# Scan quarters cut into five held pieces, one convolution tile from TensorE to VectorE, and ordered steps in the closing norm

## The chip, the core and the metric

One core of a Trainium2 chip runs the whole program. The metric is device time in microseconds (us), the median of three runs. Engines are written PE (TensorE, matrix products), DVE (VectorE), ACT (ScalarE), POOL (GpSimd) and SP (SyncE, which issues the loads). SBUF is the on-chip memory of the operands; PSUM holds the banks into which TensorE adds.

## The reference, cut to what matters

512 positions, 1024 channels. A hybrid layer comes first (block 1), and a second block of two layers follows, which the change does not touch.

```python
proj = einsum("bld,de->ble", rms_norm(x, pre_g), w_in)
conv_in, z_c, u_s, z_s, g_c, g_s = split(proj)
cu = ca * sigmoid(cb)                        # conv_in in two halves, 1024 channels
cu = causal_depthwise_conv(cu, conv_w)       # 31 taps along the positions, per channel
cu = silu(layer_norm(cu))
conv_out = (cu * silu(z_c)) @ w_conv_out
y = gelu(s5_mimo(u_s, ...))                  # 32 groups: s_t = A s_{t-1} + B u_t, complex, 64 states
y = y * sigmoid(y @ w_glu + b_glu)
ssm_out = (y * silu(z_s)) @ w_ssm_out
merged = sigmoid(g_c) * conv_out + sigmoid(g_s) * ssm_out
out = x + rms_norm(merged @ w_out, post_g)
```

## The kernel before, in words

Everything is transposed: 128 channels stand on the partitions and the 512 positions along the free side, so 1024 channels are eight tiles. A float32 product of 128x128 by 128x512 is made of three matmuls (helper `mm3`, L247 to L249: high x by high w, low x by high w, high x by low w). So each weight chunk of 128x1024 is loaded by SP (`raw`), rounded by ScalarE (`wh`, L235), and the rest is taken by VectorE (`wl`, L236), in rings of two and three buffers. A step that projects one pair of channel tiles is two banks of 24 matmuls.

Block 1 is a list of steps in ORDER_A and then ORDER_B, strings of a letter and a number. `p` projects a pair and gates it into `cu`, the input of a convolution tile on ScalarE, GpSimd or VectorE. `P` projects the same and lays it out for TensorE (`vb`, `ca`, `cp`, `cph`, `cpl`; L694 to L722). `t` is the convolution of one tile on TensorE (`toeplitz`): four weight chunks, 96 matmuls of 128x256 into one bank. `c` is the convolution of one tile tap by tap: for tiles in CONV_POOL ScalarE multiplies (`cw`, L755) and GpSimd adds into `xa` (L756), 30 times; for others VectorE does one multiply-add for each tap. `u` projects the scan's input, `s` and `z` the gates' inputs. `T` makes the scan's tables on small tiles, `R` the rotations (L506 to L511, VectorE), `Q` the kernel matrices of one quarter of the groups (outer products on GpSimd, L529 and L532; transposes and products on TensorE, L542 and L551), `q` the scan of the quarter itself: `pv` from `us` (L581), `vs` rotated through a permutation on TensorE (L585), the scan on VectorE into `st` (L591), a second permutation (L593), `sh` (L599), and sixteen products `py` (L603, L604). After that come `L`, the layer norm over all eight convolved tiles, and `C`, the projection of the convolved branch.

The order of the instructions on each engine is settled when the program is built. A scheduler that works with costs of its own takes what is ready in the order of priorities; steps get theirs in the order of the string, and B1_PRIO adds 20000 to a `c` step, so that its taps go where an engine would else be free. On the chip each engine then works its list strictly in that order. A step that is late on one engine holds what stands behind it there.

The layer ends with a norm in halves of 256 positions: for each half eight `og` multiplies (L921), eight additions (L922), eight roundings `xh` (L924) and eight rests `xl` (L925), which the next block's first matmuls read; then sums of squares of the new `x` (ScalarE squares, GpSimd adds into `acc`), which the ones-matmul L277 turns into the next norm's factor.

Of the kernel before, what the change touches and what calls it, by code (L numbers as in the profile page):

```python
# [19 lines left out]
PI_C3 = float(np.float32(TWO_PI - PI_C1 - PI_C2))  # L20
PI_CLAMP = 3.1415925

CONV_PE = (1, 2, 4, 6, 7)
VEC = {}
_o = 0
for _n, _w in (
# [466 lines left out]
def s5_rot(P, tb):  # L493
    V = P.nc.vector
    c, s = (P.q4.tile([128, 2048], F32, name=n).rearrange("p (g k) -> p g k", g=32) for n in ("rc", "rsn"))
    V.memset(c[:, :, 0:1], 1.0)
    V.memset(s[:, :, 0:1], 0.0)
    ta, tb_ = P.t("ra"), P.t("rb")
    for i in range(6):
        m = 1 << i  # L500
        n = min(32, 512 // m)
        for g0 in range(0, 32, n):
            g = slice(g0, g0 + n)
            cq, sq = (a[:, g].unsqueeze(2).to_broadcast([128, n, m]) for a in tb["rot"][i])
# [6 lines left out]
            V.tensor_tensor(out=s[:, g, m:2 * m], in0=A, in1=B, op=ALU.add)  # L511
    tb["cs"] = c, s


def s5_pre(P, tb, q):
    nc = P.nc
    V, GP = nc.vector, nc.gpsimd

    def big(name, n=1024):
        return P.q4.tile([128, n], F32, name=name, bufs=1 if name == "t1" else 2)  # L520

    def outer(out, x0, p0, x1, p1, n0, n1):
        n = n1 - n0
# [36 lines left out]

def s5_main(P, tb, q, u_dram, y_dram):
    nc = P.nc
# [13 lines left out]
    def flat(a):  # L576
        return a.rearrange("p g k -> p (g k)")
# [45 lines left out]
def block1(P, nxt):  # L623
    nc, tc, ap = P.nc, P.tc, P.ap
    V, GP, A = nc.vector, nc.gpsimd, nc.scalar
    TT = V.tensor_tensor
    STT = V.scalar_tensor_tensor
    with ExitStack() as ctx:
# [31 lines left out]
        def proj(i):  # L660
            h, l = P.wload(ap["w_in"][i], 2048)
            out = []
            for a in range(2):
                ps = P.ps()
                P.mm3(ps, h, l, 1024 * a, P.xh, P.xl)
                out.append(ps)
            return out

# [56 lines left out]
        def toeplitz(k):  # L725
# [3 lines left out]
            for c in range(4):  # L729
                (h,), (l,) = P.wload(src[:, 1024 * c:1024 * c + 1024], 1024)  # L730
                g, s0 = c // 2, 8 * (c % 2)
                for i in range(8):
                    s = 16 - s0 - i
                    o = slice(128 * i, 128 * i + 128)
                    a, b = s0 + i == 0, s0 + i == 15
                    d = ps[:, 256 * g:256 * g + 256]
                    xh, xl = hi[:, g, s:s + 256], lo[:, g, s:s + 256]
                    nc.tensor.matmul(d, h[:, o], xh, start=a, stop=False)  # L738
                    nc.tensor.matmul(d, h[:, o], xl, start=False, stop=False)
                    nc.tensor.matmul(d, l[:, o], xh, start=False, stop=b)  # L740
# [6 lines left out]
            summed(k)  # L747

        def conv(k):
            cu, y = cus[k], yc[k]  # L750
            if k in CONV_POOL:
                A.activation(y, cu[:, 0:T], AF.Identity, scale=hcw[:, 31 * k:31 * k + 1], bias=P.v("conv_b", k))
# [102 lines left out]
        def cout(o):  # L855
# [9 lines left out]
        tb = {}  # L865
        step = {"p": pair, "c": conv, "P": phases, "t": toeplitz, "u": u_, "s": zs_, "z": zc_, "g": gate, "y": gelu,
                "Q": lambda q: s5_pre(P, tb, q), "q": lambda q: s5_main(P, tb, q, u_dram, y_dram),
                "T": lambda i: tb.update(s5_tables(P, None)), "R": lambda i: s5_rot(P, tb), "G": lambda i: glu(), "S": ssm, "L": lambda i: ln(),
                "C": cout}

# [46 lines left out]
        for st, s in zip(sts, HALVES):  # L917
            A.activation(sd[:, s], st[:, s], AF.Sqrt, scale=1.0 / D, bias=P.eps6)
            V.reciprocal(rp[:, s], sd[:, s])
            for k in range(8):  # L920
                TT(out=og[k][:, s], in0=og[k][:, s], in1=rp[:, s], op=ALU.mult)  # L921
                TT(out=P.x[k][:, s], in0=og[k][:, s], in1=P.x[k][:, s], op=ALU.add)  # L922
                g = gcol(P, *nxt, k)
                A.activation(P.xh[k][:, s], P.x[k][:, s], AF.Copy, scale=g)  # L924
                STT(out=P.xl[k][:, s], in0=P.x[k][:, s], scalar=g, in1=P.xh[k][:, s].bitcast(F32), op0=ALU.mult, op1=ALU.subtract)  # L925
        for k in range(8):
            acc = P.sumsq(P.x[k], acc)
        P.rs = P.rstd_of(acc)


# [3 lines left out]
def proj_first(P, src, xT, sqx):  # L934
# [33 lines left out]
    for a in range(2):  # L968
# [8 lines left out]
B1_CLASS = {"c": "C", "t": "V", "R": "T", "T": "T", "Q": "Q", "q": "S", "y": "S", "G": "S", "L": "L"}  # L977
# [1010 lines left out]
```

## Time and profile before

| what | us |
| --- | --- |
| median of three runs | 2697.33 (2696.21 to 2700.18) |
| profiled execution | 2696.53, its span 2694.8, granted clock 0.965 |
| TensorE busy in the span | 2553.4 (95%) |
| block 1, from the first tables to the z steps, 95.5 to 372.8 | 277.30, TensorE busy 201.72 |
| z, gates and projections, 372.8 to 609 | 236.20, TensorE busy 235.31 |
| closing norm and the first half banks behind it, 609 to 638 | 29.00, TensorE busy 21.83 |

A stage's length less TensorE's busy time is what TensorE waits for there. The profiled execution's own time is 1.7 us longer than its span and lies 0.8 below the median.

### The profile page before, as it was taken

The page shows a single profiled execution, that of the slowest core. Times are in us where ns is not written, and L with a number is a line of the kernel's source. Part 1 is how long each engine was busy: PE and PEld are TensorE (multiplying, and loading weights), DVE is VectorE, ACT ScalarE, POOL GpSimd, SP SyncE. Part 2 cuts the span into 40 slices and gives each one's busy share as a digit, 9 for nine tenths or more (in the row PEclk, how much of TensorE's full clock was granted, in tenths as well). Part 3 has the DMA queues.
Part 4 walks back from the last instruction along what each step waited for, and adds up shares of the span by engine and source line. Part 5 has one row for each costly group of instructions (what it writes and reads, how often), then busy time and mean ns, then how long its engine had stood idle before and what let it go on. Part 6 is the DMA issues. An engine that isn't in the chain of part 4 may idle for free.

```text
span 2694.8 us, 32197 instructions
## 1 busy us (share of the span) xinstructions
PE 2553.4 (95%) x12828; PEld 2080.7 (77%) x12828; DVE 1432.3 (53%) x1916; ACT 947.8 (35%) x1356; POOL 511.2 (19%) x362
## 2 busy tenths in 40 slices
PE   8578789998999999999999999999999988999999
PEld 6557678887888886688678888888888767788887
DVE  7875545738434458734464344443444776643442
ACT  6443434434222233322142232432233565432231
POOL 5876702011000055332010000100001231100000
PEclk9788889999999999999899999999999989999999
DMA  4222332332232342315122332332323422132323
GB/s 145 90 83 75 94 92 86 110 118 78 92 104 95 98 142 74 79 46 124 48 78 89 99 102 87 101 102 88 108 90 126 110 90 71 52 105 85 108 92 99
DMA packets 116807, 252.91 MB, mean 94 GB/s; under 512 B 44177, under 2 KB 53137, under 8 KB 116657
## 3 DMA queue, kind: packets, MB, share of 16 engines
q1 hardware_dynamic: 116512, 250.64, 29.6%
q8 instruction: 100, 1.64, 0.2%
q14 instruction: 51, 0.41, 0.1%
q10 hardware_dynamic: 144, 0.22, 0.0%
HBM read 236.26 MB, written 13.37 MB: 93 GB/s over the span
## 4 chain that ended last, share of the span: by engine, by line
PE 70%; DVE 4%; ACT 1%; issue 1%; DMA 0%; POOL 0%; POOLq 0%; ACTq 0%; DVEq 0%
PE bank L247 21%; PE bank L248 21%; PE bank L249 21%; PE bank L1863 1%; PE bank L1225 1%; PE bank L1421 1%; PE bank L1424 0%; PE bank L1361 0%; DVE xl L270 0%; PE bank L1288 0%; PE bank L1370 0%; PE bank L1301 0%; PE bank L1366 0%; DVE xl L925 0%; PE bank L1458 0%
## 5 line engine op out<-in xcount | busy, mean ns | idle before, releaser
L235 ACT CAST wh<-raw 128x1024 fp32r<-128x1024 f32 (+1 forms) x452 | 436.8, 967 | 1225.3 <-PE bank L248 884.9
L247 PE MATMUL bank<-xh,wh 128*128 128x512 f32 (+1 forms) x2152 | 838.0, 391 | 20.7 <-ACT xh L953 6.4
L248 PE MATMUL bank<-xl,wh 128*128 128x512 f32 (+1 forms) x2152 | 838.6, 390 | 4.6 <-DVE xl L925 3.1
L249 PE MATMUL bank<-xh,wl 128*128 128x512 f32 (+1 forms) x2152 | 837.2, 390 | 0.9 <-DVE wl L236 0.9
L236 DVE TENSOR_TENSOR wl<-raw,wh 128x1024 fp32r<-128x1024 f32 (+1 forms) x418 | 485.7, 1163 | 369.3 <-ACT wh L235 360.8
L247 PEld LDWEIGHTS bank<-xh,wh 128*128 128x128 f32 x2152 | 407.3, 190 | 112.9 <-issue 10.4
L248 PEld LDWEIGHTS bank<-xl,wh 128*128 128x128 f32 x2152 | 408.0, 190 | 92.0 <-DVE xl L954 4.3
L249 PEld LDWEIGHTS bank<-xh,wl 128*128 128x128 f32 x2152 | 408.0, 190 | 86.4 <-issue 3.3
L264 POOL TENSOR_TENSOR acc<-acc,sq 128x512 f32<-128x512 f32 x54 | 89.3, 1654 | 1376.2 <-ACT sq L263 1369.4
L248 PE MATMUL bank<-ml,wh 128*128 128x512 f32 x704 | 273.9, 389 | 0.0
L249 PE MATMUL bank<-mh,wl 128*128 128x512 f32 x704 | 273.9, 389 | 0.0
L247 PE MATMUL bank<-mh,wh 128*128 128x512 f32 x704 | 272.6, 389 | 0.0
L331 DVE TENSOR_TENSOR up<-bank,rs 128x512 f32<-128x512 f32 x88 | 60.8, 691 | 273.6 <-PE bank L249 273.6
L327 DVE TENSOR_TENSOR gp<-bank,rs 128x512 f32<-128x512 f32 x88 | 60.8, 691 | 177.4 <-PE bank L249 177.1
L247 PEld LDWEIGHTS bank<-mh,wh 128*128 128x128 f32 x704 | 132.1, 188 | 27.5
L248 PEld LDWEIGHTS bank<-ml,wh 128*128 128x128 f32 x704 | 132.1, 188 | 27.5
L249 PEld LDWEIGHTS bank<-mh,wl 128*128 128x128 f32 x704 | 132.1, 188 | 27.3
L756 POOL TENSOR_TENSOR xa<-xa,cw 128x512 f32<-128x512 f32 x90 | 136.9, 1522 | 45.9 <-ACT cw L755 42.6
L236 POOL TENSOR_TENSOR wl<-raw,wh 128x1024 fp32r<-128x1024 f32 x34 | 83.0, 2443 | 143.8 <-ACT wh L235 138.5
L738 PE MATMUL bank<-cph,wh 128*128 128x256 f32 x160 | 51.8, 324 | 41.0 <-ACT cph L721 41.0
L339 DVE SCALAR_TENSOR_TENSOR xa<-bank,xa 128x512 f32<-128x512 f32 x64 | 44.3, 692 | 79.8 <-PE bank L249 79.8
L755 ACT ACTIVATE cw<-cu,hcw 128x512 f32<-128x512 f32 x90 | 63.8, 719 | 49.3 <-POOL xa L756 49.2
(642 smaller groups left out, 2967.3 us busy)
## 6 DMA issues: line engine op xcount, KB each, us to landing
raw<-in_ffn_gu_dram SPq DMA_DIRECT2D x176, 512.0 KB, 3.4
raw<-in_ffn_dn_dram SPq DMA_DIRECT2D x64, 512.0 KB, 3.5
raw<-in_w_in_dram SPq DMA_DIRECT2D x46, 512.0 KB, 3.5
raw<-in_even_in_dram SPq DMA_DIRECT2D x26, 512.0 KB, 3.5
raw<-in_ffn_dn_dram SPq DMA_DIRECT2D x64, 192.0 KB, 2.3
raw<-in_conv_dram SPq DMA_DIRECT2D x20, 512.0 KB, 3.8
xa<-in_xT_dram SPq DMA_DIRECT2D x16, 256.0 KB, 4.4
raw<-in_w_co_dram SPq DMA_DIRECT2D x8, 512.0 KB, 3.3
```

Source lines behind the costliest of these rows:

```text
L235: nc.scalar.copy(h[:, :m], raw[:, :m])
L236: self.wlo.tensor_tensor(out=l[:, :m], in0=raw[:, :m], in1=h[:, :m].bitcast(F32), op=ALU.subtract)
L247: self.nc.tensor.matmul(ps, h[i][:, s], xh[k], start=a, stop=False)
L248: self.nc.tensor.matmul(ps, h[i][:, s], xl[k], start=False, stop=False)
L249: last = self.nc.tensor.matmul(ps, l[i][:, s], xh[k], start=False, stop=b)
L264: nc.gpsimd.tensor_tensor(out=acc, in0=acc, in1=sq, op=ALU.add)
L327: nc.vector.tensor_tensor(out=gp, in0=pg, in1=rs, op=ALU.mult)
L331: nc.vector.tensor_tensor(out=up, in0=pu, in1=rs, op=ALU.mult)
L339: nc.vector.scalar_tensor_tensor(out=P.x[o], in0=ps, scalar=0.5, in1=P.x[o], op0=ALU.mult, op1=ALU.add)
L738: nc.tensor.matmul(d, h[:, o], xh, start=a, stop=False)
L755: A.activation(w, cu[:, j:j + T], AF.Copy, scale=hcw[:, 31 * k + j:31 * k + j + 1])
L756: GP.tensor_tensor(out=y, in0=y, in1=w, op=ALU.add)
```

## The change

One tile leaves TensorE: tile 7 is convolved on VectorE, and so is tile 5, which was on ScalarE and GpSimd. GpSimd keeps tiles 0 and 3, TensorE 1, 2, 4 and 6. `Q` becomes `Q` (outer products) and `K` (transposes and products); `q` becomes `q` (to `vs`), `r` (to the scan), `x` (to `sh`) and `w` (`py` and out). Each piece but `Q` is given an order edge: on TensorE it stands behind the last matmul of the step that is written ahead of it (`P.last_mm`). A convolution on GpSimd gets an edge behind the last outer product, one on VectorE an edge behind the last rotation. In the norm the multiply of `og` for tile k stands behind `xl` of tile k-3, and the sums of squares behind the last `xh`. An order edge (`tc.issue_after`) fixes who stands first in one engine's list; it is no wait between engines.

```diff
-CONV_PE = (1, 2, 4, 6, 7)
+CONV_PE = (1, 2, 4, 6)
...
-CU_BUFS = 2
-CONV_POOL = (0, 3, 5)
+CU_BUFS = 4
+CONV_POOL = (0, 3)
...
-            GP.tensor_tensor(out=o, in0=o, in1=tmp, op=ALU.add)
+            P.last_gp = GP.tensor_tensor(out=o, in0=o, in1=tmp, op=ALU.add)
...
         def conv(k):
+            with tc.issue_after((P.last_gp if k in CONV_POOL else P.last_dve).ins):
+                conv_(k)
...
+        def chain(kind, q):
+            if kind in "Qq":
+                gens[kind, q] = s5_pre(P, tb, q) if kind == "Q" else s5_main(P, tb, q, u_dram, y_dram)
+            g = gens["Q" if kind in "QK" else "q", q]
+            if kind == "Q":
+                next(g, None)
+            else:
+                with tc.issue_after(P.last_mm.ins):
+                    next(g, None)
...
+            done = []
             for k in range(8):
-                TT(out=og[k][:, s], in0=og[k][:, s], in1=rp[:, s], op=ALU.mult)
+                with tc.issue_after(done[k - 3].ins) if k > 2 else ExitStack():
+                    TT(out=og[k][:, s], in0=og[k][:, s], in1=rp[:, s], op=ALU.mult)
...
-        for k in range(8):
-            acc = P.sumsq(P.x[k], acc)
+        with tc.issue_after(xh.ins):
+            for k in range(8):
+                acc = P.sumsq(P.x[k], acc)
...
-ORDER_A = "p0 P1 c0 p3 t1 u0 u1 T c3 P2 t2 s0 s1 Q0 P4 R0 t4 p5 q0 c5 Q1 P6 q1 t6 Q2 P7 q2 t7 Q3 q3"
+ORDER_A = ("p0 P1 p3 t1 u0 u1 T Q0 P2 R0 K0 t2 Q1 c0 q0 K1 s0 r0 P4 x0 q1 Q2 s1 w0 r1 K2 p5 c3 x1 q2 Q3 t4 w1 r2 K3 P6 c5 "
+           "x2 q3 t6 w2 r3 p7 x3 w3 c7")
```

Three places show what this does to the lists of the engines. On TensorE, before, the first scan quarter stands as follows (`us` the quarter's input, `vs` the states ahead of the scan, `perm` the permutation; the matmuls of L249 close the bank of a projection):

```order
L249 MATMUL bank1_74<-xh7_99,wl_1430 128x512
L581 MATMUL bank5_78<-us_1742,m1_1379 128x64 x8
L585 MATMUL bank6_79<-vs_1759,perm_929 128x512
L603 MATMUL bank5_78<-us_1742,tz_1390 128x64
L542 MATMUL bank6_79<-ident_85,t1_1892 128x128 x4
L738 MATMUL bank7_80<-cph_1492,wh_1547 128x256
```

And now, for the same quarter (L587 was L585, L596 was L593, L607 and L608 were L603 and L604):

```order
L249 MATMUL bank1_74<-xh7_99,wl_1333 128x512
L587 MATMUL bank4_77<-vs_1280,perm_837 128x512
L247 MATMUL bank2_75<-xh0_92,wh_1401 128x512
...
L249 MATMUL bank3_76<-xh7_99,wl_1408 128x512
L596 MATMUL bank5_78<-st5_1398,perm_837 128x512
L247 MATMUL bank0_73<-xh0_92,wh_1523 128x512
...
L249 MATMUL bank1_74<-xh7_99,wl_1530 128x512
L607 MATMUL bank4_77<-us_1263,tz_993 128x64
L608 MATMUL bank4_77<-sh_1477,w2_849 128x64
```

The permutation no longer stands right behind the product whose result it rotates; between each two pieces of a quarter there are now the 48 matmuls of a projection, some with small products of the next quarter among them.

On VectorE, before, these rows stand from the second projection of tile 6 (`vb`, `ca`) to `cpl`, which tile 6's convolution on TensorE reads (`kt` is a quarter's kernel matrix):

```order
L694 TENSOR_TENSOR vb_2013<-bank1_74,rsl_297 128x512
L696 TENSOR_TENSOR ca_2014<-bank0_73,rsl_297 128x512
L236 TENSOR_TENSOR wl_2152<-raw_2150,wh_2151 128x1024
L715 SCALAR_TENSOR_TENSOR cp_2018<-vb_2013,ca_2014 64x256 x4
L555 TENSOR_TENSOR kt_1923<-kt_1923,idd_909 16x4x16
L722 TENSOR_TENSOR cpl_2024<-cp_2018,cph_2023 128x2x256
```

And now, the rows ahead of the same `cpl` (L769 is a tap of tile 5, from `cu` into `xa`; L698 was L694, L726 was L722):

```order
L769 SCALAR_TENSOR_TENSOR xa_91<-cu_1731,hcw_299,xa_91 128x512 x3
L556 TENSOR_TENSOR kt_2043<-kt_2043,idd_817 16x4x16
L769 SCALAR_TENSOR_TENSOR xa_91<-cu_1731,hcw_299,xa_91 128x512 x2
L698 TENSOR_TENSOR vb_2133<-bank1_74,rsl_297 128x512
L700 TENSOR_TENSOR ca_2134<-bank0_73,rsl_297 128x512
L769 SCALAR_TENSOR_TENSOR xa_91<-cu_1731,hcw_299,xa_91 128x512
L600 TENSOR_TENSOR vr_2024<-bank6_79,rsn_935 128x8x63
L601 TENSOR_TENSOR st5_2028<-st5_2028,rc_934 128x8x63
L236 TENSOR_TENSOR wl_2271<-raw_2269,wh_2270 128x1024
L719 SCALAR_TENSOR_TENSOR cp_2138<-vb_2133,ca_2134 64x256 x4
...
L726 TENSOR_TENSOR cpl_2144<-cp_2138,cph_2143 128x2x256
```

Tile 5's taps now stand among the rows that feed TensorE: from the `sh` of the second quarter to this `cpl` there are 26 of the 31, with six `wl`, four `cp` and the second half of a scan quarter.

On GpSimd, before, at the scan's tables (`s5bb` and the like are tables; L756 is a tap of a convolution):

```order
L756 TENSOR_TENSOR xa_91<-xa_91,cw_936 128x512
L756 TENSOR_TENSOR xa_91<-xa_91,cw_939 128x512
L365 TENSOR_TENSOR s5bb_827<-s5b_761,s5t14_811 128x512
L365 TENSOR_TENSOR s5bbs_828<-s5b_762,s5t14_811 128x512
L756 TENSOR_TENSOR xa_91<-xa_91,cw_942 128x512
L365 TENSOR_TENSOR s5tb_829<-s5b_762,s5t15_812 128x512
```

And now, at the same tables:

```order
L679 TENSOR_TENSOR sqa_121<-sqa_121,sq_183 128x512
L723 MEMSET cph_1470 128x2x16
L723 MEMSET cpl_1471 128x2x16
L365 TENSOR_TENSOR s5bb_735<-s5b_669,s5t14_719 128x512
L365 TENSOR_TENSOR s5bbs_736<-s5b_670,s5t14_719 128x512
L365 TENSOR_TENSOR s5tb_737<-s5b_670,s5t15_720 128x512
```

Before, 33 taps of the convolution stand ahead of the first table row of GpSimd; now none does, and the first comes behind the outer products of the second quarter.

## Rows read from the trace of the kernel before

**Rows 1.** The page, busy time of each engine, with its share and instructions:

```profile
PE 2553.4 (95%) x12828; PEld 2080.7 (77%) x12828; DVE 1432.3 (53%) x1916; ACT 947.8 (35%) x1356; POOL 511.2 (19%) x362
```

**Rows 2.** Windows: length, then PE, PEld, DVE, ACT, POOL busy, clock, DMA:

```profile
45.00:95.50 50.50, 46.50 (x247) 39.33 (x245) 33.32 (x34) 33.05 (x46) 46.28 (x34) 1.00 0.41 128
95.50:123.20 27.70, 0.04 (x1) 0.04 (x1) 27.47 (x61) 6.15 (x15) 21.10 (x16) 0.55 0.19 57
95.50:372.80 277.30, 201.72 (x1073) 172.16 (x1073) 177.03 (x205) 105.97 (x156) 174.58 (x132) 0.83 0.26 78
372.80:609.00 236.20, 235.31 (x1066) 195.29 (x1066) 128.00 (x159) 103.23 (x143) 22.09 (x14) 0.99 0.31 104
609.00:638.00 29.00, 21.83 (x149) 19.94 (x150) 27.45 (x51) 14.15 (x30) 9.46 (x7) 0.88 0.11 37
```

**Rows 3.** TensorE's waits, 95.5 to 372.8: us, times, longest:

```profile
PE bank L738 <- ACT cph L721: 39.5, 3, 27.7
PE bank L593 <- DVE st L591: 6.9, 3, 4.3
PE bank L740 <- DVE wl L236: 5.5, 1, 5.5
PE bank L551 <- ACT m L543: 5.0, 1, 5.0
PE bank L542 <- DVE vr L587: 4.9, 1, 4.9
```

**Rows 4.** Timeline of TensorE, tile 2's convolution: start, us, then the instruction:

```profile
123.16 0.58 PE L738 MATMUL bank<-cph,wh 128*128 128x256 f32 x1 [27.69 <-ACT cph L721]
...
125.13 0.41 PE L738 MATMUL bank<-cph,wh 128*128 128x256 f32 x1
125.34 0.41 PE L739 MATMUL bank<-cpl,wh 128*128 128x256 f32 x1
...
130.01 0.28 PE L740 MATMUL bank<-cph,wl 128*128 128x256 f32 x1
130.12 0.28 PE L738 MATMUL bank<-cph,wh 128*128 128x256 f32 x1
```

**Rows 5.** Timeline of VectorE, ahead of tile 2's convolution:

```profile
53.86 2.09 DVE L236 TENSOR_TENSOR wl<-raw,wh 128x1024 fp32r<-128x1024 f32 x1 [1.68 <-ACT wh L235]
...
89.69 1.27 DVE L411 TENSOR_SCALAR s5t<-pr 128x32 f32<-128x32 f32 x1
...
123.14 0.69 DVE L722 TENSOR_TENSOR cpl<-cp,cph 128x512 fp32r<-128x512 f32 x1
```

**Rows 6.** Timeline of VectorE, single rows beside a busy and an idle GpSimd:

```profile
153.53 2.25 DVE L236 TENSOR_TENSOR wl<-raw,wh 128x1024 fp32r<-128x1024 f32 x1
...
159.24 1.77 DVE L510 TENSOR_TENSOR rb<-rc,rs 128x512 f32<-128x512 f32 x1
...
226.02 1.23 DVE L236 TENSOR_TENSOR wl<-raw,wh 128x1024 fp32r<-128x1024 f32 x1 [4.13 <-ACT wh L235]
...
234.13 0.69 DVE L703 SCALAR_TENSOR_TENSOR cu<-vb,ca 128x512 f32<-128x512 f32 x1
...
250.08 5.66 DVE L715 SCALAR_TENSOR_TENSOR cp<-vb,ca 64x256 f32<-64x256 f32 x4
```

**Rows 7.** GpSimd's taps, by source (min/median/max ns), then by line, 95.5 to 372.8:

```profile
L756 POOL TENSOR_TENSOR xa<-xa,cw x90: 1253/1305/2876, 38.7 to 317.9; 128x512 f32<-128x512 f32 x90
...
L756 POOL TENSOR_TENSOR xa<-xa,cw 128x512 f32<-128x512 f32 x58 | 86.6, 1494 | 23.3 <-ACT cw L755 22.0
```

**Rows 8.** Closing norm: TensorE's first waits, and VectorE's rows:

```profile
613.51 0.73 PE L247 MATMUL bank<-xh,wh 128*128 128x256 f32 x3 [3.26 <-ACT xh L924]
617.32 0.58 PE L248 MATMUL bank<-xl,wh 128*128 128x256 f32 x1 [3.07 <-DVE xl L925]
...
608.69 2.76 DVE L921 TENSOR_TENSOR og<-og,rp 128x256 f32<-128x256 f32 x8
...
625.33 10.61 DVE L925 SCALAR_TENSOR_TENSOR xl<-xa,vec,xh 128x256 fp32r<-128x256 f32 x8
```

More of the change, by code (lines that the diff above doesn't have):

```diff
@@ L510, in s5_rot @@
             V.tensor_tensor(out=B, in0=c[:, g, 0:m], in1=sq, op=ALU.mult)
-            V.tensor_tensor(out=s[:, g, m:2 * m], in0=A, in1=B, op=ALU.add)
+            P.last_dve = V.tensor_tensor(out=s[:, g, m:2 * m], in0=A, in1=B, op=ALU.add)
     tb["cs"] = c, s
@@ L537, in s5_pre @@
     outer(w2, tb["bc"][2], tb["spr"], tb["bc"][3], tb["npi"], 0, 9)
+    yield
     m1 = big("m1").rearrange("p (g s) -> p g s", g=8)
@@ L583, in s5_main @@
     nc.scalar.copy(vs, pv)
+    yield
     pw_ = P.side("pvs")
@@ L591, in s5_main @@
     V.tensor_tensor_scan(out=st, data0=flat(d0), data1=vs, initial=0.0, op0=ALU.mult, op1=ALU.add)
+    yield
     p2 = P.side("pss")
@@ L599, in s5_main @@
     V.tensor_tensor(out=sh[:, :, 1:64], in0=st3[:, :, 0:63], in1=vr3[:, :, 0:63], op=ALU.subtract)
+    yield
     py = P.side("py")
@@ L664, in proj @@
                 ps = P.ps()
-                P.mm3(ps, h, l, 1024 * a, P.xh, P.xl)
+                P.last_mm = P.mm3(ps, h, l, 1024 * a, P.xh, P.xl)
                 out.append(ps)
@@ L739, in toeplitz @@
                     nc.tensor.matmul(d, h[:, o], xl, start=False, stop=False)
-                    nc.tensor.matmul(d, l[:, o], xh, start=False, stop=b)
+                    P.last_mm = nc.tensor.matmul(d, l[:, o], xh, start=False, stop=b)
             y3 = y.rearrange("p (k o) -> p o k", o=2)
@@ L749, in conv, with conv_ @@
         def conv(k):
+            with tc.issue_after((P.last_gp if k in CONV_POOL else P.last_dve).ins):
+                conv_(k)
+        def conv_(k):
             cu, y = cus[k], yc[k]
@@ L863, in cout @@
             STT(out=P.xl[o], in0=P.x[o], scalar=0.5, in1=P.xh[o].bitcast(F32), op0=ALU.mult, op1=ALU.subtract)
-        tb = {}
+        tb, gens = {}, {}
+        def chain(kind, q):
[7 more added lines that the diff above has]
+                    next(g, None)
         step = {"p": pair, "c": conv, "P": phases, "t": toeplitz, "u": u_, "s": zs_, "z": zc_, "g": gate, "y": gelu,
-                "Q": lambda q: s5_pre(P, tb, q), "q": lambda q: s5_main(P, tb, q, u_dram, y_dram),
+                **{n: (lambda q, n=n: chain(n, q)) for n in "QKqrxw"},
                 "T": lambda i: tb.update(s5_tables(P, None)), "R": lambda i: s5_rot(P, tb), "G": lambda i: glu(), "S": ssm, "L": lambda i: ln(),
@@ L919, in block1 @@
             V.reciprocal(rp[:, s], sd[:, s])
+            done = []
             for k in range(8):
-                TT(out=og[k][:, s], in0=og[k][:, s], in1=rp[:, s], op=ALU.mult)
+                with tc.issue_after(done[k - 3].ins) if k > 2 else ExitStack():
+                    TT(out=og[k][:, s], in0=og[k][:, s], in1=rp[:, s], op=ALU.mult)
                 TT(out=P.x[k][:, s], in0=og[k][:, s], in1=P.x[k][:, s], op=ALU.add)
                 g = gcol(P, *nxt, k)
-                A.activation(P.xh[k][:, s], P.x[k][:, s], AF.Copy, scale=g)
-                STT(out=P.xl[k][:, s], in0=P.x[k][:, s], scalar=g, in1=P.xh[k][:, s].bitcast(F32), op0=ALU.mult, op1=ALU.subtract)
-        for k in range(8):
-            acc = P.sumsq(P.x[k], acc)
+                xh = A.activation(P.xh[k][:, s], P.x[k][:, s], AF.Copy, scale=g)
+                done.append(STT(out=P.xl[k][:, s], in0=P.x[k][:, s], scalar=g, in1=P.xh[k][:, s].bitcast(F32),
+                                op0=ALU.mult, op1=ALU.subtract))
+        with tc.issue_after(xh.ins):
+            for k in range(8):
+                acc = P.sumsq(P.x[k], acc)
         P.rs = P.rstd_of(acc)
@@ L974 @@
          ("w", 1, slice(0, 512)), ("x", 3, None), ("w", 1, slice(512, 1024)), ("x", 4, None), ("x", 5, None), ("x", 6, None), ("x", 7, None))
-ORDER_A = "p0 P1 c0 p3 t1 u0 u1 T c3 P2 t2 s0 s1 Q0 P4 R0 t4 p5 q0 c5 Q1 P6 q1 t6 Q2 P7 q2 t7 Q3 q3"
+ORDER_A = ("p0 P1 p3 t1 u0 u1 T Q0 P2 R0 K0 t2 Q1 c0 q0 K1 s0 r0 P4 x0 q1 Q2 s1 w0 r1 K2 p5 c3 x1 q2 Q3 t4 w1 r2 K3 P6 c5 "
+           "x2 q3 t6 w2 r3 p7 x3 w3 c7")
 ORDER_B = "z0 z1 z2 z3 y0 g0 g1 g2 y1 y2 y3 g3 G L g4 g5 g6 S0 g7 S1 C0 C1 C2 C3 C4 C5 C6 C7"
-B1_CLASS = {"c": "C", "t": "V", "R": "T", "T": "T", "Q": "Q", "q": "S", "y": "S", "G": "S", "L": "L"}
+B1_CLASS = {"c": "C", "t": "V", "R": "T", "T": "T", "Q": "Q", "K": "Q", "q": "S", "r": "S", "x": "S", "w": "S", "y": "S", "G": "S", "L": "L"}
 B1_PRIO = {"A": 0, "T": 0, "Q": 0, "S": 0, "C": 20000, "V": 0, "L": 0, "Z": 50000}
-CU_BUFS = 2
-CONV_POOL = (0, 3, 5)
+CU_BUFS = 4
+CONV_POOL = (0, 3)
 EVEN_IN = ["even_in", "lora", "g_up", "even_out"]
```

## The prediction

> **What bounds the kernel now.** The page's first part comes first [rows 1]: TensorE is busy 95% of the span, every other engine 53% or less. So a gain must come from matmuls left out or from TensorE's idle time, 141 us over the span. The windows say where that lies [rows 2]. From 372.8 to 609 TensorE is busy 235.3 of 236.2 us, and nothing that another engine does faster or slower there shows unless it becomes very late. From 95.5 to 372.8 it is busy 201.7 of 277.3: 75.6 us idle, over half of all of it, in the stage that the change rewrites. The granted clock there is 0.83, against 1.00 and 0.99 in the stages on both sides. The closing norm has 7.2 us idle in 29.
>
> The view of waits names what TensorE waited for in the long stage [rows 3]. The largest part is 39.5 us for `cph`, the operand of a convolution on TensorE: 27.7 of it ahead of tile 2, 11.8 in two more, of which tile 7's is the larger. Tile 2's wait is the whole window 95.5 to 123.2, in which VectorE is busy 27.47 of 27.70 [rows 2]: it works through the scan's tables, and tile 2's `cp` and `cpl` come at their end [rows 5]. The other rows are of a few us: a fourth weight chunk of tile 2 that comes late on VectorE (`wl`, 5.5), the scan (`st`, 6.9 in three), the transposes (5.0 and 4.9). These are waits for results that had been started just ahead of the matmul that reads them.
>
> **The change, part by part.**
>
> *Tile 7 leaves TensorE.* 96 matmuls. On TensorE two of them start 0.21 us apart at the beginning of tile 2, and 0.12 later [rows 4]: these are the two clock levels, so 96 cost 11.4 us at the high and 20 at the low. I take 13, since the stage's mean clock is 0.83 (11.4/0.83 is 13.7) but tile 7 stood near its end. Its wait (the larger part of 11.8) goes with it.
>
> *The front.* GpSimd is busy 46.28 of 50.5 us from 45 to 95.5 [rows 2], nearly all of it taps of tile 0, and these now stand behind the tables (the last place shown in the order). Beside them a `wl` on VectorE takes 2.09 instead of 1.23, and 1.77 is what a two-input row takes where 0.69 is its price alone [rows 5, 6]. TensorE is idle 4.0 us there; I give back half: it ends this stage at 93.5, not 95.5. The tables on VectorE are mostly rows of 32 or 64 columns that depend on one another and gain little more. Before, tile 2 starts at 123.16 [rows 4]; I put `cpl` at 117.1: 2 from the front and 4.1 from taps and their table rows on GpSimd that no longer hold what VectorE reads. That makes the first wait 23.6 where it was 27.7.
>
> *The pieces.* Between the product and the permutation that reads it stand 48 matmuls of a projection now (first place in the order): by 0.22 each (235.31/1066 in the next window [rows 2]) they are 10.6 us of cover, against waits that were 2 to 5. So the waits for `m`, `vr`, `st` at the three first quarters go, about 17 us of [rows 3]. What is late next: tile 2's fourth `wl`, which stands behind 24 rotation rows on VectorE, while GpSimd now has outer products without a break: 8.5, where it was 5.5; the first `x` piece 4.5, since the scan there stands behind the last rotations; the first `w` 1.5. GpSimd's own list: the second half of the third quarter's `w2` stands, from the first `d0` row on, behind some 56 instructions. Before, they take about 1.5 each (86.6 us for 58 taps [rows 7]), and a tap is idle 0.4 on the average for ScalarE (23.3/58). From 119.8 that is 84 + 24 x 0.4, so 214; TensorE gets to that read at 205 to 209. I take 9, in two pieces.
>
> *Tile 5 on VectorE.* This is the large one. Of its 31 taps 26 stand between the second `sh` and `cpl` of tile 6 (second place). With them: six `wl`, four `cp`, and fourteen rows of the scan and of `kt`. What does a tap cost there? A row with two inputs from SBUF takes 0.69 with GpSimd idle and 1.77 beside GpSimd; a `wl` 1.23 and 2.25; the four `cp` 5.66 beside it, by the same ratio 2.2 alone [rows 6]. Alone the whole list is 26 x 0.69 + 6 x 1.23 + 2.2 + some 6 for the fourteen = 33 us. Beside GpSimd it is 26 x 1.75 + 6 x 2.2 + 5.7 + some 18 = 82. GpSimd is busy 174.6 of 277.3 us before [rows 2] and has less free time in the middle now, when tiles 0 and 3 and the outer products fall together; I take a quarter of the 49 us between the two as free of it, 12: 70. TensorE has 32 us of its own there (the last 80 matmuls of tile 4 at 0.12, a projection of 10.6, and two scan pieces, transposes and products, some 12). So 36 to 38 us idle; I take 36, spread over tile 4's last chunk, the second bank of tile 6's projection, the third `x`, and mostly ahead of tile 6's convolution.
>
> *Tile 7 on VectorE* (31 rows by 0.69, 21 us) comes behind the quarters, in a stage in which GpSimd has 22 us of work in 236 and VectorE 128 [rows 2]. It is needed by the layer norm, far behind; I cost it at nothing. The cover is the z and gate projections; without it, it would cost its 21 us. *CU_BUFS 4* costs memory alone.
>
> *The norm.* Before, all eight `og` are multiplied ahead of the first `xl` [rows 8]; now three are. At 0.345 each (2.76/8) five rows less is 1.7 us for the first `xh`, and the first `xl` gains up to its 3.07. The last eight `xl` took 10.61 us beside GpSimd's sums, 1.33 each for rows of half the width; the sums now follow the last `xh`. The work of VectorE is the same in sum, and it is busy 27.45 of 29.0 [rows 2], so not all of the 6.3 us of the two waits can be had: between 0 and 6.3, I take 2.5. The sums end later, by some 4 us, but the ones-matmul that reads them stands behind banks that need no norm factor yet.
>
> *Sum.* Idle: 23.6 + 8.5 + 4.5 + 1.5 + 9 + 36 = 83, where it was 75.6. Busy: 201.7 - 13 = 189. The stage ends at 93.5 + 83 + 189 = 365.5, not 372.8: 7.3 less. With the norm 9.8. The profiled execution then takes 2696.53 - 9.8 = 2686.7, and the median, 0.8 above it before, about 2687.
>
> **The rivals.** *A: the taps of tile 5 cost TensorE little.* If VectorE's taps go at 0.69 to 1.0 in that stretch (because GpSimd is not busy, or takes its own turn later), the list is 33 to 40 us for TensorE's 32, and the 36 us shrink to 5 or less: 2655. For it: 226.02 and 234.13, where `wl` and a row of two inputs have their low prices in the middle of the same stage [rows 6]. Against it: GpSimd is given the outer products and 60 taps in that stage, and they now come later than before. *B, slower: each row of VectorE waits for a whole tap.* In the stretch ahead of tile 6's `cpl` a row then costs its own price and 1.25, the least of a tap [rows 7]: taps 26 x 1.94, `wl` 6 x 2.48, `cp` 6.4, the fourteen others 18.5, in sum 90 and not 70. That is 20 us more idle ahead of tile 6: 2707. For it: 2.25 for a `wl` and 5.66 for four `cp` are near it already [rows 6]. Against it: 1.77 for a row of 0.69 is less than 1.94, and a GpSimd that waits for ScalarE (23.3 us in 58 taps [rows 7]) leaves gaps. It decides if tile 6's convolution starts over 185 us behind tile 2's; the forecast has it some 173 behind.
>
> The Trainium skill, page "SBUF — State Buffer", section "Who interferes with whom", has the rule of B: a VectorE instruction with two SBUF inputs contends with a GpSimd instruction that reads SBUF, and the loser is blocked for the whole of the other. The trace agrees in kind, with 1.77 for 0.69, and not to the full; by the rule the time is B's.
>
> *C: late convolutions hold the layer norm.* GpSimd ends its 60 taps some 205 us behind tile 2's start, at about 322, and VectorE has tile 7's 21 us to do in a stage where it is busy 128 of 236 [rows 2]; the norm stands behind the z and most gate projections, by my estimate 80 us later than that. It would need a loss of 80 us to matter; I give it no chance of its own.
>
> **How the numbers follow.** The forecast 0.50, with 2675 to 2700 as its own range (contention from half to full); A 0.28; B 0.22. About 0.2%, 5.4 us, is what a measurement tells from no change: faster is below 2691.9, slower above 2702.7. Faster: 0.32 of the forecast's 0.50 and all of A, 0.60. Same: 0.16 of the forecast and 0.04 of B, 0.20. Slower: 0.02 and 0.18, 0.20. The range reaches down to 2650, just past A, and up to 2708, just past B.
>
> **What would show it.** In the profile after: TensorE's wait ahead of tile 2 near 23.6 us; no wait for `vs` or `vr` in the first quarters; the taps of tile 5 on VectorE at a mean of about 1.6 (A: under 1.0) and a wait of TensorE ahead of tile 6's convolution of over 15 us for `cph` or `cpl`; a wait for GpSimd's `w2` at the third quarter; the stretch from the z steps as before; the norm's idle time at 4 to 5. The prediction is wrong if VectorE is not late with its list (A), or if the clock falls further with the longer waits: it is 0.55 in the window of the 27.7 us wait [rows 2] and starts at the low level behind it [rows 4], so a wait of over 20 us ahead of tile 6 would cost some 3 us more by slow matmuls.

## The result, and the profile after

| | median of four runs, us | range | profiled span, clock |
| --- | --- | --- | --- |
| before | 2698.22 | 2696.21 to 2700.18 | 2694.8, 0.965 |
| changed | 2676.95 | 2672.12 to 2679.15 | 2674.7, 0.962 |

The changed kernel takes 0.9919 of the time (95% interval 0.9902 to 0.9936): 21 us less, where the prediction had 10 less and a range that holds it. The trace shows that this is a sum of two numbers, neither of which was forecast. The place to cut the program is the ones-matmul that closes block 1, ahead of the norm. The two rows below are its second half on TensorE's timeline, the first of the kernel before (L914), the second of the changed one (L933):

```profile
609.55 0.48 PE L914 MATMUL bank<-sq,ones 128*128 128x256 f32 x1 [0.87 <-ACT sq L910]
```

```profile
566.44 0.48 PE L933 MATMUL bank<-sq,ones 128*128 128x256 f32 x1 [0.87 <-ACT sq L929]
```

Block 1 ends 43.1 us earlier. What lies behind it, source that the change does not touch but for the norm (the rest, from here on), took 2694.8 - 609.55 = 2085.3 us and now takes 2674.7 - 566.44 = 2108.3: 23.0 us longer. So the parts have to be read one by one.

**Block 1.** Windows of the changed kernel (columns as in [rows 2]); the second is the wait ahead of tile 2, and the next four go on from there; the z steps begin at 332.4, in the last one:

```profile
45.00:89.94 44.94, 44.94 (x244) 38.82 (x242) 25.62 (x62) 14.51 (x23) 5.13 (x6) 1.00 0.47 154
89.94:108.57 18.63, 0.00 (x1) 0.00 (x1) 17.05 (x29) 3.73 (x6) 11.77 (x10) 0.56 0.21 63
108.57:180.00 71.43, 60.55 (x310) 50.12 (x311) 64.87 (x71) 26.45 (x37) 57.52 (x42) 0.88 0.25 73
180.00:240.00 60.00, 50.86 (x301) 43.08 (x300) 48.54 (x38) 31.35 (x46) 57.97 (x40) 0.93 0.24 67
240.00:300.00 60.00, 38.70 (x216) 32.16 (x215) 55.35 (x47) 27.36 (x40) 49.75 (x30) 0.75 0.29 85
300.00:352.00 52.00, 51.07 (x240) 42.23 (x239) 47.43 (x63) 22.91 (x32) 13.69 (x10) 1.00 0.36 111
```

TensorE never waits from 45 on and is free at 89.94 (95.48 before), with GpSimd busy 5 us of 45 there, not 46 of 50. The wait ahead of tile 2 is 18.6, not 27.7. From there to 180 VectorE is busier than TensorE, from 180 to 240 GpSimd is, and from 240 to 300 VectorE again, where the clock is 0.75 and TensorE is idle 21 us. The view of TensorE's waits, 89 to 372, answers to [rows 3]:

```profile
PE bank L742 <- ACT cph L725: 32.2, 2, 18.6
PE bank L744 <- DVE wl L236: 8.3, 2, 5.9
PE bank L552 <- POOL w L532: 5.1, 3, 2.4
PE bank L587 <- ACT m L544: 4.8, 1, 4.8
PE bank L543 <- ACT yq L610: 3.0, 1, 3.0
PE bank L543 <- POOL tz L546: 2.5, 1, 2.5
PE bank L596 <- DVE st L593: 2.3, 1, 2.3
```

Besides tile 2's 18.6 the first row holds 13.6 ahead of tile 6. The whole way to the ones-matmul, first before, then changed, and the changed kernel from TensorE's last matmul ahead of tile 2 to the z steps:

```profile
0.00:609.55 609.55, 520.82 (x2524) 434.48 (x2524) 375.39 (x454) 271.06 (x387) 262.69 (x202) 0.92 0.31 99
```

```profile
0.00:566.44 566.44, 497.27 (x2428) 411.90 (x2428) 413.76 (x508) 244.62 (x347) 233.55 (x171) 0.94 0.32 102
...
89.94:332.40 242.46, 181.59 (x976) 151.35 (x977) 213.71 (x215) 100.75 (x145) 190.70 (x129) 0.85 0.27 78
```

TensorE is idle 69.2 us up to the ones-matmul and was 88.7: that is 19.6 of the 43.1. The other 23.5 is busy time: 96 matmuls are gone (tile 7's), and the mean granted clock is 0.94 where it was 0.92.

**Tile 5's stretch.** The second `sh` ends at 215.5 and tile 6's `cpl` at 276.9. One window of the changed kernel, and VectorE's groups by line in it (busy and mean in ns):

```profile
215.50:276.90 61.40, 35.24 (x193) 28.11 (x192) 60.87 (x52) 25.14 (x38) 52.09 (x32) 0.77 0.23 66
```

```profile
L769 DVE SCALAR_TENSOR_TENSOR xa<-cu,hcw,xa 128x512 f32<-128x512 f32 x26 | 33.3, 1280 | 0.5
L236 DVE TENSOR_TENSOR wl<-raw,wh 128x1024 fp32r<-128x1024 f32 x6 | 12.9, 2144 | 0.0
```

The list is the forecast one: 26 taps, six `wl`, VectorE busy 60.9 of 61.4. A tap costs 1.28 in the mean and not 1.75, beside a GpSimd that is busy 85%. That mean is of two prices. Here are the 26 by source (min/median/max in ns), and two groups of them on VectorE's timeline:

```profile
L769 DVE SCALAR_TENSOR_TENSOR xa<-cu,hcw,xa x26: 732/1638/1775, 217.1 to 276.8; 128x512 f32<-128x512 f32 x26
```

```profile
227.80 10.96 DVE L769 SCALAR_TENSOR_TENSOR xa<-cu,hcw,xa 128x512 f32<-128x512 f32 x7
...
262.87 1.52 DVE L769 SCALAR_TENSOR_TENSOR xa<-cu,hcw,xa 128x512 f32<-128x512 f32 x2
```

Of the 26, 11 took 0.73 to 0.75 us and 15 took 1.59 to 1.78, with none between.

**The second block.** TensorE's list differs there, though the source is the same: counted by names and shapes in the trace, some 300 of the 2270 matmuls of one stage stand in another order, and some 60 outside it. In this stage the second block's recurrent layer mixes products of 64x64 and 32x32 with projections of 512 columns. I take it that the scheduler comes to that stage with other engines free first; the experiments test the list, not that reason. The stage's window, first before, then changed, and a piece of the changed one:

```profile
1063.56:1303.91 240.35, 236.66 (x2270) 185.41 (x2268) 129.20 (x208) 60.51 (x96) 74.69 (x40) 0.98 0.32 82
```

```profile
1018.33:1284.32 265.99, 255.75 (x2271) 200.12 (x2269) 133.60 (x212) 61.66 (x98) 78.01 (x40) 0.90 0.28 74
...
1218.00:1238.00 20.00, 19.67 (x174) 17.26 (x175) 8.72 (x18) 0.00 (x0) 0.00 (x0) 0.51 0.39 117
```

The same 2270 matmuls take 25.6 us more: 6.5 more idle time and 19 more busy time at a clock of 0.90 for 0.98. In the piece from 1218 TensorE is busy 98% of the time and yet at 0.51, the low one of its two levels. Two rows of its timeline stand ahead of that, the second the beginning of a run of small products with few wide ones between:

```profile
1196.45 0.80 PE L247 MATMUL bank<-cr,wh 128*128 128x512 f32 x1 [3.97 <-DVE c L1521]
1218.33 0.90 PE L1312 MATMUL bank<-xl,xa 64*64 64x64 f32 x7 [0.94 <-DVE xl L1309]
```

**The norm.** Its waits answer to [rows 8]:

```profile
568.73 0.62 PE L247 MATMUL bank<-xh,wh 128*128 128x256 f32 x3 [1.58 <-ACT xh L945]
570.82 0.58 PE L248 MATMUL bank<-xl,wh 128*128 128x256 f32 x1 [1.48 <-DVE xl L946]
...
581.44 0.39 PE L248 MATMUL bank<-xl,wh 128*128 128x256 f32 x1 [0.97 <-DVE xl L946]
```

### The profile page after: what moved, and what is told of

It reads as the page before. It is cut to its first block, busy times and chain, and to the rows that moved or that the text cites. A ratio compares the mean times of both kernels' runs of the same rounds, so it can differ in the third digit from the quotient of the medians.

```text
span 2674.7 us, 31936 instructions
## 1 busy us (share of the span) xinstructions
PE 2550.5 (95%) x12732; PEld 2075.1 (78%) x12732; DVE 1466.0 (55%) x1970; ACT 921.8 (34%) x1316; POOL 485.4 (18%) x331
## 4 chain that ended last, share of the span: by engine, by line
PE 79%; DVE 9%; POOL 3%; issue 2%; ACT 2%; DMA 1%; SPq 0%; DVEq 0%; ACTq 0%; POOLq 0%
PE bank L247 24%; PE bank L248 24%; PE bank L249 23%; POOL xa L764 1%; DVE wl L236 1%; DVE xa L769 1%; PE bank L1887 1%; POOL acc L264 1%; PE bank L1445 0%; PE bank L1249 0%; DMA b<-td 0%; PE bank L1448 0%; ACT wh L235 0%; DMA s<-nd 0%; PE bank L1312 0%
## 5 line engine op out<-in xcount | busy, mean ns | idle before, releaser
L235 ACT CAST wh<-raw 128x1024 fp32r<-128x1024 f32 x448 | 432.9, 967 | 1225.0 <-PE bank L248 918.0
L249 PE MATMUL bank<-xh,wl 128*128 128x512 f32 (+1 forms) x2152 | 840.9, 392 | 0.2 <-DVE wl L236 0.2
L236 DVE TENSOR_TENSOR wl<-raw,wh 128x1024 fp32r<-128x1024 f32 (+2 forms) x414 | 480.5, 1161 | 327.4 <-ACT wh L235 324.8
L249 PEld LDWEIGHTS bank<-xh,wl 128*128 128x128 f32 x2152 | 411.0, 191 | 89.5 <-issue 5.5
L249 PE MATMUL bank<-mh,wl 128*128 128x512 f32 x704 | 273.9, 389 | 0.0
L249 PEld LDWEIGHTS bank<-mh,wl 128*128 128x128 f32 x704 | 132.2, 188 | 27.4
L764 POOL TENSOR_TENSOR xa<-xa,cw 128x512 f32<-128x512 f32 x60 | 101.4, 1691 | 10.3 <-ACT cw L763 7.6
L253 ACT CAST mh<-m 128x512 fp32r<-128x512 f32 x88 | 55.0, 626 | 58.7 <-DVE m L333 58.7
L742 PE MATMUL bank<-cph,wh 128*128 128x256 f32 x128 | 39.4, 308 | 32.2 <-ACT cph L725 32.2
```

What stands on the lines that cost most here:

```text
L235: nc.scalar.copy(h[:, :m], raw[:, :m])
L236: self.wlo.tensor_tensor(out=l[:, :m], in0=raw[:, :m], in1=h[:, :m].bitcast(F32), op=ALU.subtract)
L249: last = self.nc.tensor.matmul(ps, l[i][:, s], xh[k], start=False, stop=b)
L253: self.nc.scalar.copy(hi, src)
L764: GP.tensor_tensor(out=y, in0=y, in1=w, op=ALU.add)
```

## The experiments

In each the theory and a rival were given numbers first. Ratios are to runs of the kernel before made beside them, with the 95% interval.

**e1: no edges on the norm's multiplies.**

```diff
-                with tc.issue_after(done[k - 3].ins) if k > 2 else ExitStack():
+                with ExitStack():
```

> The changed kernel without the edges on the norm's multiplies (all else kept, the sums of squares too). In the changed kernel the ones-matmul that closes block 1 starts 43.1 us earlier than before (566.4 for 609.6), and the rest of the program, whose source is not touched, takes 23.0 us longer (2108.3 for 2085.3); in the second block TensorE's list of small products and projections is another one. Without these edges that list is again the one of before, but for one row in 3200. Theory 'the list of the second block': the rest takes 2085 to 2090 and the whole some 2656, 20 us less than the changed kernel. Rival 'a denser first block is paid back by the clock later, whatever the list': the rest stays at 2108 and the whole at 2677 to 2680.

2659.56 us (2656.79 to 2660.45), 0.9865 [0.9850, 0.9880]: 17 us less than the changed kernel. Block 1 ends at 566.85 and the rest takes 2088.2; the recurrent stage:

```profile
1020.61:1266.28 245.67, 238.52 (x2270) 186.41 (x2268) 132.38 (x209) 60.70 (x96) 73.55 (x40) 0.97 0.30 80
```

Of the 23.0 us lost behind block 1, 20 come back when edges in the norm, far ahead of that stage, are taken out.

**e2: the norm's edges alone, on the kernel before** (both edges of the change's last part, nothing else).

```diff
+                with tc.issue_after(done[k - 3].ins) if k > 2 else ExitStack():
...
+        with tc.issue_after(xh.ins):
```

> The kernel before with the norm's edges alone. Its list in the second block is then near that of the changed kernel. Theory 'the list': the first block as before (609 to 610), the norm's first waits 2 to 3 us shorter, the rest some 20 us longer, 2715 in all. Rival 'denser first block': the rest as before or 2.5 us less, 2695 to 2698.

2713.64 us (2706.62 to 2730.74), 1.0083 [1.0051, 1.0115]. Block 1 is the one of before (the same ones-matmul at 609.69), the rest takes 2102.2, 17 more than before, and the recurrent stage 257.6 us:

```profile
1063.17:1320.78 257.61, 248.43 (x2271) 193.56 (x2270) 137.05 (x213) 61.85 (x98) 78.11 (x40) 0.93 0.29 77
```

The loss is there without a denser block 1, and in e1 a denser block 1 is there without most of the loss. That rival is out.

**e3: tile 5's taps later in the order string.**

```diff
- ... P6 c5 x2 q3 t6 w2 r3 p7 x3 w3 c7
+ ... P6 x2 q3 t6 w2 r3 p7 x3 w3 c5 c7
```

> The changed kernel with the taps of tile 5 on VectorE behind the last scan quarter, ahead of those of tile 7; the list of the second block is that of the changed kernel. The prediction's term (26 taps beside GpSimd ahead of tile 6's operand): the 26 us idle on TensorE between the second w piece and the start of tile 6's convolution shrink to 8 or less, block 1 ends 15 to 20 us earlier, 2658 in all. Rival 'it is not the taps but GpSimd's own list and the loads that make tile 6 late': under 5 us less, 2672 to 2677.

2674.28 us (2663.95 to 2675.49), 0.9911 [0.9885, 0.9936], as the changed kernel. It tests nothing: the taps stood where they had stood, since a `c` step's priority fills VectorE's free places wherever the letter is.

**e4: tile 7 again on TensorE.**

```diff
-CONV_PE = (1, 2, 4, 6)
+CONV_PE = (1, 2, 4, 6, 7)
...
- ... p7 x3 w3 c7
+ ... P7 x3 w3 t7
```

> The changed kernel with tile 7 again prepared for and convolved on TensorE (96 matmuls, as the last step of the order with the fourth w). By the prediction's term it costs 11.4 to 13 us and its operand's wait as far as it is not covered: block 1 ends 12 to 16 us later, 2689 to 2693 in all. Rival 'the matmuls fill time in which TensorE would wait': 2677 to 2682.

2697.54 us, 1.0007 [0.9976, 1.0037], with runs in two groups (2684 to 2689 and 2706 to 2712; the profile is of the first). In the profile the first banks behind the norm come 27.7 us later than in the changed kernel, about double the forecast; the rest is then 19 shorter than in the changed kernel, 2089.3. The median lies above both expectations, between its two groups. One wait makes up 9.4 of the 27.7, the last quarter's `w` (0.9 in the changed kernel):

```profile
PE bank L608 <- DVE sh L602: 10.3, 1, 10.3
```

**e5: tile 5's and 7's taps held behind the scan**, on e1.

```diff
-    V.tensor_tensor(out=sh[:, :, 1:64], ...)
+    P.last_dve = V.tensor_tensor(out=sh[:, :, 1:64], ...)
...
- ... P6 c5 x2 q3 t6 w2 r3 p7 x3 w3 c7
+ ... P6 x2 q3 t6 w2 r3 p7 x3 w3 c5 c7
```

> The kernel of e1 (no edges on the norm's multiplies) with the taps of tiles 5 and 7 on VectorE held by an edge behind the last scan quarter's last row, so that none of the 26 taps stands ahead of tile 6's operand. In e3 the place in the order string alone had left 25 of them there, since the priority of a c step lets its taps fill VectorE's free places in the scheduler's own reckoning; so e3 told nothing of this term. Prediction's term: the 14 us wait at tile 6 and the small ones in the same stretch shrink to under 8 together, block 1 ends 12 to 20 us earlier than in e1, 2640 to 2648 in all. Rival 'GpSimd's list and the loads make tile 6 late': under 5 us, 2655 to 2660. Rival 'the layer norm now waits': later than e1.

2644.55 us (2636.73 to 2646.24), 0.9801 [0.9784, 0.9817]: 15 less than e1. Tile 6 starts 14.6 us earlier than in e1 (275.2), on TensorE's timeline:

```profile
260.58 0.58 PE L742 MATMUL bank<-cph,wh 128*128 128x256 f32 x1 [7.67 <-ACT cph L725]
```

Block 1 ends 16.9 earlier, nearly all of it idle time (53.8 us for 68.6). The waits in the stretch do not fall under 8 together: besides the 7.7 there are 3.7 and 2.4 for GpSimd's `w`. The taps cost TensorE time as the prediction had it; their place was a choice.

**e6: the front alone, on the kernel before** (an edge holds the three GpSimd convolutions behind the outer products).

```diff
-ORDER_A = "p0 P1 c0 p3 t1 u0 u1 T c3 P2 t2 s0 s1 Q0 P4 R0 t4 p5 q0 c5 Q1 ...
+ORDER_A = "p0 P1 p3 t1 u0 u1 T Q0 P2 t2 s0 s1 c0 P4 R0 t4 p5 c3 q0 c5 Q1 ...
```

> The kernel before with its three convolutions on GpSimd behind the outer products of the scan, four buffers, nothing else; the second block's list is that of before row for row. Theory 'the front': the scan's tables on VectorE and GpSimd no longer stand beside taps, TensorE is free at 90 and tile 2 starts at 109 instead of 123, some 14 us earlier; of that the later taps give something back beside tiles 4 and 6: 2682 to 2690 in all. Rival 'the prediction's 6 us': tile 2 starts at 117 and the whole is 2690 to 2697.

2685.39 us (2684.79 to 2685.85), 0.9957 [0.9941, 0.9974]. Tile 2 starts 1.0 us later than in the changed kernel. Of TensorE's waits in the kernel before, these two stood behind it:

```profile
PE bank L585 <- ACT vs L583: 4.2, 1, 4.2
PE bank L581 <- DMA us<-u_dram: 3.7, 1, 3.7
```

In e6 both are larger, on TensorE's timeline:

```profile
109.59 0.58 PE L738 MATMUL bank<-cph,wh 128*128 128x256 f32 x1 [18.59 <-ACT cph L721]
...
182.37 1.22 PE L585 MATMUL bank<-vs,perm 128*128 128x512 f32 x1 [11.32 <-ACT vs L583]
...
239.98 0.45 PE L581 MATMUL bank<-us,m 128*128 128x64 f32 x1 [7.12 <-DMA us<-u_dram]
```

13.6 us are won and 12 kept, as the theory had it.

**e7: no edges on the scan's pieces**, on e1.

```diff
-                with tc.issue_after(P.last_mm.ins):
-                    next(g, None)
+                next(g, None)
```

> The kernel of e1 without the edges on TensorE of the scan's pieces (K, q, r, x, w): same steps in the same order of priorities, the pieces free to be placed where the scheduler has them ready. If the edges carry the pieces' gain, waits of 4 to 5 us for vs, vr and st come back, 10 to 17 us in all, and the time is 2668 to 2677. If the order of the steps alone gives it: 2655 to 2663.

2664.58 us (2658.75 to 2665.20), 0.9876 [0.9861, 0.9890], between the two expectations. One chain wait of the old kind comes back, at the fourth quarter:

```profile
268.26 1.22 PE L587 MATMUL bank<-vs,perm 128*128 128x512 f32 x1 [6.22 <-ACT vs L584]
```

But TensorE waits less elsewhere, 55.2 us up to the z steps for 60.7 in e1; its matmuls take 9 us more (busy 507.5 for 498.2 up to the ones-matmul, at 0.93 for 0.94). That the edges are worth 5 us is not shown: the intervals touch.

**e8: tile 5 on GpSimd**, on e1.

```diff
-CONV_POOL = (0, 3)
+CONV_POOL = (0, 3, 5)
```

> The kernel of e1 with tile 5's taps on ScalarE and GpSimd again (behind the outer products), 90 taps there as before. VectorE is then free of the 26 taps ahead of tile 6, but GpSimd's list is 46 us longer. If VectorE's taps are the price, tile 6's wait falls to under 5 us and the whole is 2642 to 2650; if contention with GpSimd's taps comes back later or GpSimd's own kernel matrices are late, 2655 to 2665.

2671.05 us (2666.69 to 2675.37), 0.9904 [0.9889, 0.9920]: slower than both expectations. Tile 6 starts at 259.4, 16 earlier than in e1, and still waits 6.3, but `wl` is late in the z steps, beside GpSimd's later taps:

```profile
PE bank L249 <- DVE wl L236: 12.8, 5, 3.2
```

Block 1 ends 8.8 later than in e1, and the rest takes 9.8 more, which nothing here explains.

**e9: the sums' edge undone** in the changed kernel, the multiplies' edges kept.

```diff
-        with tc.issue_after(xh.ins):
-            for k in range(8):
-                acc = P.sumsq(P.x[k], acc)
+        for k in range(8):
+            acc = P.sumsq(P.x[k], acc)
```

> The changed kernel with its edges on the norm's multiplies kept, and only the edge of the sums of squares undone. The list of the second block is then near that of before (3152 of 3200 rows stand in the same order, 2724 with that of the changed kernel). Theory 'the list': the rest of the program behind the norm takes 2085 to 2093 us again, and the whole is 2655 to 2662, though the edges that e1 took out are there. Rival 'the edges on the multiplies cost the time themselves': 2675 to 2680 as in the changed kernel.

2662.79 us (2661.31 to 2665.35), 0.9877 [0.9860, 0.9893]: within 1 us of the theory of the list, with the edges that e1 took out in place. The rest takes 2095.0, 2 above the theory's range: 13 of the 23 us come back. The recurrent stage takes 245.6 us at 0.97.

**e10: the norm as before**, both edits of it undone in the changed kernel.

```diff
-                with tc.issue_after(done[k - 3].ins) if k > 2 else ExitStack():
...
-        with tc.issue_after(xh.ins):
```

> The changed kernel with the whole norm as before, both kinds of edges undone. Its list in the second block is near that of the changed kernel (3037 of 3200 rows; 2847 with that of before), without any edge in the norm. Theory 'the list': the rest takes 15 to 25 us longer than in e1, 2673 to 2685 in all. Rival 'the edges cost it': 2657 to 2663.

2660.27 us (2658.55 to 2666.28), 0.9871 [0.9853, 0.9888]: the theory's number missed, the rival's met. The rest takes 2090.0. The recurrent stage is longer than e1's and e9's, but by 7 us only:

```profile
1017.92:1270.92 253.00, 245.19 (x2271) 190.19 (x2270) 133.32 (x213) 61.91 (x98) 77.42 (x40) 0.95 0.30 78
```

So a list near the changed kernel's by the count of rows does not cost the whole 26 us.

**e11 and e12: tile 0, then tile 3, too, on VectorE behind the scan**, on e5.

```diff
-CONV_POOL = (0, 3)
+CONV_POOL = (3,)
...
+CONV_POOL = ()
```

> The kernel of e5 with tile 0's taps, too, on VectorE behind the last scan quarter, so that GpSimd has 30 taps instead of 60 beside the scan's rows. If what is left of TensorE's waits up to tile 6 is GpSimd's list and its contention with VectorE (w 3.7 and 2.4, cph 7.7 in e5), 8 to 14 us go and the whole is 2631 to 2638; if VectorE then is the bound in the z stage (three tiles by 23 us), or the layer norm waits, it is 2645 to 2660.

2633.46 us (2627.11 to 2636.57), 0.9764 [0.9746, 0.9783], the fastest of all, and in the forecast range, but not for the reason given: of the 11 us that block 1 ends earlier than in e5, 3 are waits (idle 50.8 for 53.8, tile 6 still waits 7.7) and 8 are busy time. The 90 late taps, by source (min/median/max in ns), with GpSimd quiet beside them:

```profile
L769 DVE SCALAR_TENSOR_TENSOR xa<-cu,hcw,xa x90: 739/746/753, 285.8 to 398.8; 128x512 f32<-128x512 f32 x90
```

In the changed kernel the same row reads:

```profile
L769 DVE SCALAR_TENSOR_TENSOR xa<-cu,hcw,xa x60: 732/752/1775, 217.1 to 359.2; 128x512 f32<-128x512 f32 x60
```

> The kernel of e11 with tile 3's taps, too, on VectorE behind the last scan quarter: no tap is left on ScalarE and GpSimd, and VectorE has four tiles by 23 us in the z and gate stage. In e11 VectorE is busy 154 of 210 us from 340 to 550 with part of three tiles. If the remaining taps on GpSimd still hold its kernel matrices and VectorE's two-input rows in the scan stage, 3 to 8 us go: 2625 to 2631. If VectorE is full in the z stage and the layer norm waits: 2640 to 2660.

2652.11 us (2648.82 to 2654.82), 0.9834 [0.9815, 0.9852]. The layer norm now waits for the last tile; TensorE's waits, 90 to 600:

```profile
PE bank L247 <- ACT cah L253: 11.2, 1, 11.2
PE bank L277 <- POOL acc L264: 9.8, 1, 9.8
```

## Why the prediction came out right, point by point

The time fell into the range and the direction held, but by errors that cancel, and that is luck. Up to the norm the sum had 7.3 us less, and 43.1 were measured; behind the norm it had nothing, and 23.0 were lost. At the z steps its 365.5 was 93.5 + 83 + 189 (front, idle, busy); the trace has 332.4, of 89.9 + 60.9 + 181.6. So the front was 3.6 too long, the idle time 22 and the busy time 7.

- **What bounds the kernel** held for block 1 in part: of the 43.1, 19.6 were idle time and 23.5 busy. It named two sources of a gain, idle time and matmuls left out; some 10 of the 23.5 are neither, since the 96 matmuls were costed at 13, and I put them to the higher granted clock. It was wrong by silence for the rest: "the source is not touched" was read as "the time is not touched", and the list of the second block was not looked at. That the norm's edges bring the loss is shown: of the 23 us e1 gets 20 back, e9 13 and e10 18, and e2 has 17 of loss without the rest of the change. That they do it by the order of TensorE's rows fits best but is not settled. For it: the stage took 240 to 249 us at 0.96 to 0.98 in the nine kernels whose list is near that of before, and 251 to 266 at 0.90 to 0.96 in the five others (e2, e3, e4, e10 and the changed one). Against it: the whole rest took 2084 to 2098 in the nine and 2089 to 2108 in the five, so the groups overlap there, and e4's runs, all of one list with all the edges, lie in groups some 25 us apart, the profiled one with next to none of the loss. The list's likeness to another, counted in rows, is no measure of it. Which rows cost the clock, and why e4's runs fall into two groups, stays open.
- **The front** was mis-sized: TensorE free at 89.9, not 93.5, and tile 2 at 108.6, not 117.1. The term gave back half of TensorE's 4.0 us idle and 4.1 us of the tables; all of the 4.0 went, and the tables lost every tap beside them. e6 shows the 13.6 us at tile 2 by itself.
- **The pieces**: where none was forecast, one of 4.8 stands ahead of the first permutation (put down to `m`, though the matmul reads `vs`); the ones forecast at the first `x` and `w` (4.5 and 1.5) are not there. Tile 2's late `wl` is 5.9 for 8.5. GpSimd's `w` holds TensorE 5.1 us in three waits for the 9 forecast, and `tz` and `yq` 5.5, which were not forecast. e7 does not show the cover by edges as such: without them one wait of 6.2 came back, for a forecast of 10 to 17.
- **Tile 5** went as the mechanism had it, and the size was off: 61.4 us for 70 between the bounds of 33 and 82. The step that was off is the quarter of the span between the bounds that it took as free of GpSimd: 61.4 is 42% of the way down from 82, and 11 of 26 taps, 42%, paid nothing. The price of a tap beside GpSimd was near: 1.59 to 1.78 for 1.75. TensorE was 26.1 us idle from the last chunk of tile 4 to tile 6 (2.4, 2.5, 1.4, 2.3, 2.4, 13.6, 1.5) for 36; 6.3 of that (2.5, 1.4 and the second 2.4) are waits for GpSimd's `tz` and `w`, counted under the pieces too. e5 shows that 15 us are to be had. Rival A fell by the trace: TensorE did wait. Its 2655 is near e1 by accident.
- **Rival B** fell by its own test: tile 6's convolution starts 166 us behind tile 2's, for its 185 and the forecast's 173. (Worked strictly by its rule its sum is 96 and not 90: the four `cp` are 7.2, the fourteen others 23.5.) A tap takes 0.75 alone; beside GpSimd 15 of 26 paid 0.85 to 1.03 more, not the 1.25 of [rows 7], and 11 paid nothing. The rule of the Trainium skill, page "SBUF — State Buffer", section "Who interferes with whom", says who is blocked by order of issue, and not that VectorE is always the one; that was B's. The two prices, up to 0.75 and from 1.59, agree with the exclusive lock that it names.
- **Tile 7** was mis-sized: 13 and a wait, against 27.7 in e4. 11.4 is matmuls, 9.4 a wait for `sh` that is not the operand's wait that the prediction had in mind (tile 7's first matmul does not wait in e4). TensorE's busy time up to the ones-matmul grows by 17.9, so 6.5 of it is more than the matmuls at the high clock; that this goes with the clock, 0.93 for 0.94, I argue, and no run takes it apart.
- **The norm**: 2.5 forecast. In the changed kernel its waits fall from 7.2 to 4.9, and against e1 the edges win 0.9 us; alone on the kernel before (e2) they lose 1.8 up to the first banks of the next block, for a wait for `wh` of 1.4 that takes their place.
- **Rival C** did not occur: with two tiles late on VectorE the layer norm waits 0.6, with three none, with four (e12) 21.

## What to carry to other kernels

When a scheduler writes the order, an edit's time is not in the edited lines alone: compare the lists of every later stage too, and cut the span at a row that both kernels have before any gain is credited. Filler work on an engine that feeds the bottleneck belongs behind that stage by an edge, not by a priority, which lets the scheduler place it by its own prices: here 25 or 26 taps that take 0.75 us alone and took 1.28 in the mean. Two errors that cancel look like a good forecast, so each term needs its own row after.

## What was not expected of the hardware

TensorE was busy 98% of a 20 us stretch and had a granted clock of 0.51 there, in a run of 64x64 and narrower products with few wide ones between (1218 to 1238 in the changed kernel). What in that run brings the clock down is not shown. The same 2270 matmuls, in one order or another, took from 240 to 266 us, at 0.98 to 0.90. And a VectorE tap beside GpSimd had two prices, some 0.74 and some 1.67 us, and none between; a mean hides that.
